# A hybrid decoder layer: the gate matrix of the expert stage built eight tokens at a time, with its products on GpSimd and ScalarE

## The chip, the cores and the metric

The kernel runs on one core of one Trainium2 chip. Its time is the device time of one execution in microseconds (us). The kernel before took 3386.84 us (median of three runs, 3384.8 to 3387.58). The five engines of the core are TensorE (PE in the profile, with PEld for its weight loads), VectorE (DVE), ScalarE (ACT), GpSimd (POOL) and SyncE (SP), which here issues nearly all DMAs.

## What is computed

The reference is one decoder layer on 512 tokens of width 2048: modulation, a short convolution beside differential attention, an output projection, and then a product-key expert layer (PEER), which is where the change lies. For every token it picks 8 x 16 of 16384 one-neuron experts:

```
idx = jnp.take_along_axis(cand_idx, top_p, axis=-1)      # 128 experts of a token
g   = jax.nn.softmax(top_s.astype(jnp.float32), axis=-1)
a   = jnp.einsum('thkd,td->thk', jnp.take(expert_u, ib, axis=0), xb)
w   = gelu(a) * gb
out = jnp.einsum('thk,thkd->td', w, jnp.take(expert_v, ib, axis=0))
```

All arithmetic that the change touches is in float32.

## The kernel before, in words

The kernel treats the first 160 tokens of the expert layer (TG) by gathering their experts' rows, and the other 352 (TD) densely: it computes the activations of all 16384 experts for them, multiplies each by its gate (zero for experts not chosen) and multiplies with all rows of expert_v. An expert's number is 128 times a high part plus a low part, so the gates of one token are a 128 x 128 matrix, G = sum over its 128 picks of onehot(high) x gate x onehot(low).

**The gate-matrix stage (lines 914 to 938)** makes G for the 352 dense tokens, in 11 blocks of 32 (GB). `opT[i]` holds, with the 128 picks on the partitions, the high part, the low part and the gate of every token; `iof` is the row 0..127. Four tokens at a time: VectorE compares `iof` with both parts (line 924, 2 x 4 x 128 elements, into a `gt` tile of which there are three); two tokens' one-hots of the high part are multiplied by the gates on VectorE (line 927) and two on ScalarE (line 930), into `og` (three buffers); TensorE multiplies the two one-hot matrices of each token (line 933, one float32 product shows as two instructions in the trace); ScalarE moves the four results out of PSUM into `gtile` (line 934; two buffers), and after 32 tokens SP stores the block to `g_dram` (line 935).

**What runs beside it.** `u_block(e)` (line 790) makes the activations of 128 experts: 48 matrix products per block (line 798). Its rows come from `u_dram`, in a half-block `u_turn` (line 777): SP loads `ur` (line 783), VectorE transposes it for blocks from 12 on (line 786), and `split` makes a high and a low half, on ScalarE (line 88) and VectorE (line 89). Blocks 0 to 3 lie before the stage, 4 to 11 belong to it. `lay_out` (line 224) issues DMAs from one place in DRAM to another, `u_dram`, 256 KB each, which have been put behind a gate product in the program's order only. The blocks need no gate matrix. The first products with expert_v (line 963) do: they take W, which `w_block` (line 823) makes from a reload of `g_dram` (line 826), over all 11 stores.

**The order of the work** on each engine is fixed when the program is built: a scheduler interleaves the stage and the blocks by its own estimate of times, under the dependencies and the explicit orders. Each engine then goes through its row in that order. PSUM has eight banks: in this stage two for the blocks (psA) and six for `pv` (psV).

Of the kernel before, what the change touches and what calls it, by code (L numbers as in the profile page):

```python
# [57 lines left out]
OG_BUFS = 3  # L58
# [20 lines left out]
def hymba_peer(tc, x, c, positions, w_ada, b_ada, norm1_g, w_in, conv_w, q_norm_g, k_norm_g,  # L79
# [18 lines left out]
    with ExitStack() as ctx:  # L98
# [663 lines left out]
        psV = psV_ctx.enter_context(tc.tile_pool(name="psV", bufs=6, space=PSUM))  # L762
# [151 lines left out]
        with tc.tile_pool(name="gs", bufs=2, side="right") as gs:  # L914
            iof = gs.tile([P, P], F32, name="iof", bufs=1)
            nc.gpsimd.iota(iof, pattern=[[1, P]], base=0, channel_multiplier=0, allow_small_or_imprecise_dtypes=True)
            nb_ = TD // GB
            for b in range(nb_):
                gt_ = gs.tile([P, NK, GB], F32, name="gtile")
                for t4 in range(0, GB, 4):  # L920
                    i, tt = divmod(TG + b * GB + t4, P)
                    o = opT[i]
                    oh = gp.tile([P, D], F32, name="gt", bufs=GBUF)[:, 0:D // 2].rearrange("p (a t n) -> p a t n", a=2, n=P)
                    nc.vector.tensor_tensor(out=oh, in0=iof[:, None, None, :].to_broadcast([P, 2, 4, P]),  # L924
                                            in1=o[:, 0:2, tt:tt + 4, None].to_broadcast([P, 2, 4, P]), op=OP.is_equal)
                    og = gs.tile([P, 4, P], F32, name="og", bufs=OG_BUFS)
                    nc.vector.tensor_tensor(out=og[:, 0:2], in0=oh[:, 0, 0:2],
                                            in1=o[:, 2, tt:tt + 2, None].to_broadcast([P, 2, P]), op=OP.mult)
                    for j in (2, 3):
                        nc.scalar.activation(og[:, j], oh[:, 0, j], AF.Copy, scale=o[:, 2, tt + j:tt + j + 1])  # L930
                    pg = psV.tile([P, 4, P], F32, name="pv")
                    for j in range(4):
                        gm = nc.tensor.matmul(pg[:, j], oh[:, 1, j], og[:, j], start=True, stop=True)  # L933
                    nc.scalar.activation(gt_[:, :, t4:t4 + 4], pg.rearrange("p t n -> p n t"), AF.Copy)
                nc.sync.dma_start(g_dram[b], gt_)
                lay_out(min(2 if b % 2 else 1, len(lay)), gm)
                if b >= nb_ - (RUN - NT):
                    u_block(RUN - nb_ + b, behind=gm if b == nb_ - 1 else None)
# [134 lines left out]
```

## Time and profile before

| | us |
|---|---|
| three runs, median | 3386.84 |
| the profiled execution, its own time | 3396.71 |
| span of its instructions | 3394.6 |
| TensorE / VectorE / ScalarE / GpSimd busy | 3183.8 / 2815.8 / 1218.1 / 1002.0 |
| one gate comparison, line 924 (88 of them) | 1.218 |
| one product on VectorE, line 927 (88) | 0.416 |

The profile is that of one execution. Busy time counts an instruction from its start to its end; two neighbours on an engine overlap a little, so busy sums run above the time that the engine needs. The granted clock of TensorE over the span is 0.976 of full speed. The gate-matrix stage lies between 1281 and 1454 us. Before it, up to 1281 us, comes the choice of the experts; behind it the long loop over all experts, to the end.

### The profile page before, as it was taken

What the parts mean: (1) busy time and instruction counts of PE and PEld (TensorE: products, weight loads), DVE (VectorE), ACT (ScalarE), POOL (GpSimd) and SP (SyncE); (2) the same over time, 40 slices, a digit from 0 to 9 for tenths busy, and PEclk for the clock granted to TensorE, in tenths of its full rate; (3) what the DMA queues carried; (4) which work ended last, traced back from release to release, by engine and by line L of the source; (5) the groups of instructions that cost most, each with busy time, mean ns of one, the idle gap of its engine ahead of it and who ended that gap; (6) DMA issues with size and microseconds to landing.
All of it is one profiled execution on the core that took longest, in us unless ns stands there. A gap on an engine that the chain in (4) does not pass through costs nothing.

```text
span 3394.6 us, 47070 instructions
## 1 busy us (share of the span) xinstructions
PE 3183.8 (94%) x18006; PEld 2947.5 (87%) x18006; DVE 2815.8 (83%) x3779; ACT 1218.1 (36%) x1826; POOL 1002.0 (30%) x665
## 2 busy tenths in 40 slices
PE   4888999999999859799999999999999999999998
PEld 3766867777878649799999999999999999999997
DVE  5879767853337998978999899999999999999975
ACT  5232333343245426643233333333333333333322
POOL 2446423344445640002223222222222222222210
PEclk9999999999999979999999999999999999999999
DMA  8875978876979868888998899998988988998964
GB/s 287 277 257 174 310 247 284 271 251 203 330 248 305 281 227 305 288 314 323 350 343 336 318 339 345 349 332 330 339 323 320 345 340 325 360 331 335 347 237 168
DMA packets 388895, 1017.80 MB, mean 300 GB/s; under 512 B 29713, under 2 KB 108478, under 8 KB 328126
## 3 DMA queue, kind: packets, MB, share of 16 engines
q1 hardware_dynamic: 342590, 679.23, 59.1%
q0 software_dynamic: 46080, 335.56, 25.3%
q8 instruction: 141, 2.31, 0.3%
q14 instruction: 84, 0.69, 0.1%
HBM read 965.11 MB, written 171.18 MB: 335 GB/s over the span
## 4 chain that ended last, share of the span: by engine, by line
PE 68%; DVE 17%; DMA 9%; issue 2%; ACT 1%; SPq 1%; POOL 1%; DVEq 0%; ACTq 0%; POOLq 0%
PE pv L963 27%; PE pa L798 27%; DMA ada_w<-in_w_ada_dram 5%; PE pm L471 5%; DVE ada_acc L196 2%; PE pm L557 2%; DVE run L196 2%; DVE gt L924 2%; PE pm L257 2%; PE pm L712 1%; DMA wraw<-in_w_out_dram 1%; PE pv L933 1%; DVE tkj L687 1%; PE sp L425 1%; DVE cv L674 1%
## 5 line engine op out<-in xcount | busy, mean ns | idle before, releaser
L798 PE MATMUL pa<-hd,ut 128*128 128x352 f32 x6144 | 1066.7, 326 | 28.7 <-DVE ut L89 21.7
L963 PE MATMUL pv<-W,vs 128*128 128x352 f32 x6144 | 1049.0, 324 | 5.8 <-ACT W L88 2.6
L798 PEld LDWEIGHTS pa<-hd,ut 128*128 128x128 f32 x6144 | 1007.3, 190 | 33.6 <-DVE ut L89 24.3
L963 PEld LDWEIGHTS pv<-W,vs 128*128 128x128 f32 x6144 | 997.9, 188 | 9.3 <-ACT W L88 3.5
L89 POOL TENSOR_TENSOR wsp<-wraw,wsp 128x1024 fp32r<-128x1024 f32 x160 | 393.6, 2464 | 559.3 <-ACT wsp L88 524.5
L88 ACT ACTIVATE vs<-vr 128x1024 fp32r<-128x1024 f32 x256 | 271.6, 1061 | 741.8 <-PE pv L963 694.8
L852 POOL DMA_INDIRECT gt<-in_expert_u_dram,idxu x128 | 181.7, 1419 | 724.4 <-DVE gt L860 318.8
L860 DVE SCALAR_TENSOR_TENSOR gt<-gt,h2n 128x2048 f32<-128x2048 f32 x160 | 364.3, 2281 | 14.9 <-DMA gt<-in_expert_u_dram,idxu 14.9
L88 ACT ACTIVATE ut<-ur 128x1024 fp32r<-128x1024 f32 x256 | 269.5, 1055 | 296.6 <-PE pa L798 229.5
L873 DVE SCALAR_TENSOR_TENSOR gacc<-gt,ga_a,gacc 128x2048 f32<-128x2048 f32 x158 | 369.5, 2339 | 3.0 <-DMA gt<-in_expert_v_dram,idxu 2.2
L89 DVE TENSOR_TENSOR vs<-vr,vs 128x1024 fp32r<-128x1024 f32 x256 | 310.7, 1214 | 53.4 <-ACT vs L88 53.0
L89 DVE TENSOR_TENSOR ut<-ur,ut 128x1024 fp32r<-128x1024 f32 x256 | 310.4, 1216 | 46.8 <-ACT ut L88 45.9
L852 POOL DMA_INDIRECT gt<-in_expert_v_dram,idxu x128 | 175.2, 1369 | 551.1 <-DVE gacc L873 382.1
L88 ACT ACTIVATE wsp<-wraw 128x1024 fp32r<-128x1024 f32 x160 | 169.1, 1058 | 389.5 <-issue 94.7
L471 PE MATMUL pm<-big,wsp 128*128 128x512 f32 x1152 | 286.5, 401 | 0.0
L786 DVE STREAM_TRANSPOSE ur<-ur 128x1024 f32<-128x1024 f32 x232 | 274.4, 1219 | 10.6 <-DMA ur<-u_dram 10.6
L471 PEld LDWEIGHTS pm<-big,wsp 128*128 128x128 f32 x1152 | 215.3, 192 | 42.9
L196 DVE SCALAR_TENSOR_TENSOR ada_acc<-ada_w,scol,ada_acc 128x512 f32<-128x512 f32 x195 | 208.1, 1067 | 39.0 <-DMA ada_w<-in_w_ada_dram 35.0
L257 PE MATMUL pqk<-wsp,big 128*128 128x512 f32 x768 | 192.0, 409 | 22.4 <-DVE qk L303 14.5
L712 PE MATMUL pm<-big,wsp 128*128 128x512 f32 x768 | 187.3, 401 | 19.5 <-POOL wsp L89 17.9
L257 PEld LDWEIGHTS pqk<-wsp,big 128*128 128x128 f32 x768 | 149.5, 198 | 58.6 <-DVE qk L303 17.4
L712 PEld LDWEIGHTS pm<-big,wsp 128*128 128x128 f32 x768 | 146.1, 193 | 52.5 <-POOL wsp L89 20.9
(271 smaller groups left out, 3045.1 us busy)
## 6 DMA issues: line engine op xcount, KB each, us to landing
ur<-u_dram SPq DMA_DIRECT2D x128, 1024.0 KB
vr<-in_expert_v_dram SPq DMA_DIRECT2D x256, 512.0 KB
u_dram<-in_expert_u_dram SPq DMA_DIRECT2D x464, 256.0 KB
ada_w<-in_w_ada_dram SPq DMA_DIRECT2D x192, 512.0 KB
wraw<-in_w_in_dram SPq DMA_DIRECT2D x96, 512.0 KB
g_dram<-gtile SPq DMA_DIRECT2D x11, 2048.0 KB
g<-g_dram SPq DMA_DIRECT2D x32, 704.0 KB
wraw<-in_w_out_dram SPq DMA_DIRECT2D x32, 512.0 KB
```

The source lines that it names most:

```text
L88: hi = nc.scalar.activation(dst[:, 0], src, AF.Copy)
L89: (eng or nc.vector).tensor_tensor(out=dst[:, 1], in0=src, in1=dst[:, 0].bitcast(F32), op=OP.subtract)
L196: nc.vector.scalar_tensor_tensor(new, wt[:, k], s, old, op0=OP.mult, op1=OP.add)
L257: nc.tensor.matmul(banks[i], hT[kk][:, a, i * P:(i + 1) * P], ws[:, b, k], start=(kk == last[0] and n == 0), stop=(kk == last[1] and n == 2))
L471: nc.tensor.matmul(banks[n2], ws[:, a, k, n2 * P:(n2 + 1) * P], hT[kk][:, b], start=(kk == 0 and n == 0), stop=(kk == KC - 1 and n == 2))
L712: nc.tensor.matmul(banks[j], ws[:, a, k, j * P:(j + 1) * P], h2T[kk][:, b], start=(kk == 0 and n == 0), stop=(kk == KC - 1 and n == 2))
L786: nc.vector.transpose(t, t)
L798: mm = nc.tensor.matmul(pa[:, :TD], ut[:, a, j].rearrange("p b r -> p (b r)"), hd[k][:, b], start=(k == 0 and n == 0), stop=(k == KC - 1 a ...
L852: d = nc.gpsimd.indirect_dma_start(out=t, out_offset=None, in_=src, in_offset=bass.IndirectOffsetOnAxis(ap=gidx[g][:, j:j + 1], axis=0))
L860: return lambda: nc.vector.scalar_tensor_tensor(t, t, 1.0, h2n, op0=OP.mult, op1=OP.mult, accum_out=ga_a[:, j:j + 1])
L873: return lambda: nc.vector.scalar_tensor_tensor(gacc, t, a, gacc, op0=OP.mult, op1=OP.add)
L963: mm = nc.tensor.matmul(pv[j // 2][:, j % 2, :TD], vs[:, a, bb, j * P:(j + 1) * P], W[e0 // 2][:, m, bb], start=(b == 0 and n == 0), stop= ...
```

## The change

The comparison takes eight tokens at once (2 x 8 x 128 elements, the whole `gt` tile). The row `iof` is still made by GpSimd in SBUF (now `ios`), and ScalarE copies it once to a PSUM bank of its own (psI); psV goes from six banks to five. The product with the gates leaves VectorE: GpSimd does six of the eight tokens in one instruction, ScalarE two (OG_ACT), one at a time as before. `og` holds eight tokens and has two buffers instead of three. The matrix products and the way out of PSUM are the same instructions, in two groups of four per comparison, the group that holds ScalarE's tokens first.

```diff
-OG_BUFS = 3
+OG_BUFS = 2
+OG_ACT = 2
...
-        psV = psV_ctx.enter_context(tc.tile_pool(name="psV", bufs=6, space=PSUM))
+        psI = psV_ctx.enter_context(tc.tile_pool(name="psI", bufs=1, space=PSUM))
+        psV = psV_ctx.enter_context(tc.tile_pool(name="psV", bufs=5, space=PSUM))
...
-            iof = gs.tile([P, P], F32, name="iof", bufs=1)
-            nc.gpsimd.iota(iof, pattern=[[1, P]], base=0, channel_multiplier=0, allow_small_or_imprecise_dtypes=True)
+            ios = gs.tile([P, P], F32, name="ios", bufs=1)
+            nc.gpsimd.iota(ios, pattern=[[1, P]], base=0, channel_multiplier=0, allow_small_or_imprecise_dtypes=True)
+            iof = psI.tile([P, P], F32, name="iof")
+            nc.scalar.activation(iof, ios, AF.Copy)
...
-                for t4 in range(0, GB, 4):
...
-                    nc.vector.tensor_tensor(out=oh, in0=iof[:, None, None, :].to_broadcast([P, 2, 4, P]),
-                                            in1=o[:, 0:2, tt:tt + 4, None].to_broadcast([P, 2, 4, P]), op=OP.is_equal)
-                    og = gs.tile([P, 4, P], F32, name="og", bufs=OG_BUFS)
-                    nc.vector.tensor_tensor(out=og[:, 0:2], in0=oh[:, 0, 0:2],
-                                            in1=o[:, 2, tt:tt + 2, None].to_broadcast([P, 2, P]), op=OP.mult)
-                    for j in (2, 3):
+                for t8 in range(0, GB, 8):
...
+                    nc.vector.tensor_tensor(out=oh, in0=iof[:, None, None, :].to_broadcast([P, 2, 8, P]),
+                                            in1=o[:, 0:2, tt:tt + 8, None].to_broadcast([P, 2, 8, P]), op=OP.is_equal)
+                    og = gs.tile([P, 8, P], F32, name="og", bufs=OG_BUFS)
+                    m = 8 - OG_ACT
+                    nc.gpsimd.tensor_tensor(out=og[:, 0:m], in0=oh[:, 0, 0:m],
+                                            in1=o[:, 2, tt:tt + m, None].to_broadcast([P, m, P]), op=OP.mult)
+                    for j in range(m, 8):
                         nc.scalar.activation(og[:, j], oh[:, 0, j], AF.Copy, scale=o[:, 2, tt + j:tt + j + 1])
...
+                    for t4 in (4, 0):
+                        pg = psV.tile([P, 4, P], F32, name="pv")
+                        for j in range(4):
+                            gm = nc.tensor.matmul(pg[:, j], oh[:, 1, t4 + j], og[:, t4 + j], start=True, stop=True)
+                        nc.scalar.activation(gt_[:, :, t8 + t4:t8 + t4 + 4], pg.rearrange("p t n -> p n t"), AF.Copy)
```

Lines below the change move down by up to six: line 798 of before is line 800 of the changed kernel, 89 is 90, 924 is 928, 933 is 939, 786 is 788, 831 is 833.

The scheduler lays the stage out anew. TensorE's row of before, at the end of the stage (L933 is the gate product, one row count per token; L798 the products of an expert block):

```order
L933 MATMUL pv<-og,gt 128x128 x4
L798 MATMUL pa<-hd_7407,ut 128x352 x2
L933 MATMUL pv<-og,gt 128x128 x8
L798 MATMUL pa<-hd_7408,ut 128x352 x3
L798 MATMUL pa<-hd_7409,ut 128x352 x3
L933 MATMUL pv<-og,gt 128x128 x188
L798 MATMUL pa<-hd_7394,ut 128x352 x3
```

The same place in the changed kernel (L939 is the gate product, L800 the block's):

```order
L939 MATMUL pv<-og,gt 128x128 x4
L800 MATMUL pa<-hd_7403,ut 128x352
L800 MATMUL pa<-hd_7404,ut 128x352 x3
L800 MATMUL pa<-hd_7405,ut 128x352
L939 MATMUL pv<-og,gt 128x128 x4
L800 MATMUL pa<-hd_7405,ut 128x352 x2
L800 MATMUL pa<-hd_7406,ut 128x352 x3
L800 MATMUL pa<-hd_7407,ut 128x352 x3
L939 MATMUL pv<-og,gt 128x128 x8
L800 MATMUL pa<-hd_7408,ut 128x352 x3
L800 MATMUL pa<-hd_7409,ut 128x352 x3
L939 MATMUL pv<-og,gt 128x128 x31
```

Before, all seven blocks come early and the last 188 tokens stand alone; now the blocks' products are spread over the stage, 341 of them between the first gate product and the last, and 31 tokens stand alone at its end. Behind the last gate product follow 98 products of blocks before, 162 now, until the first product with expert_v.

VectorE's row of before in the middle of its tail (L924 the comparison, L927 the product, L89 the low half of a block's rows, L831 the product with the reloaded gates):

```order
L924 TENSOR_TENSOR gt<-iof,opT_10381 128x1024
L927 TENSOR_TENSOR og<-gt,opT_10381 128x256 x2
L924 TENSOR_TENSOR gt<-iof,opT_10381 128x1024 x2
L927 TENSOR_TENSOR og<-gt,opT_10381 128x256
L924 TENSOR_TENSOR gt<-iof,opT_10381 128x1024
L927 TENSOR_TENSOR og<-gt,opT_10381 128x256 x2
L89 TENSOR_TENSOR ut<-ur,ut 128x1024 x2
L831 TENSOR_TENSOR W<-W,g_12008 128x704 x2
```

VectorE's row at the end of the changed stage (L928 the comparison, L90 the low half, L788 the transposes):

```order
L928 TENSOR_TENSOR gt<-iof,opT_10384 128x2048 x3
L90 TENSOR_TENSOR ut<-ur,ut 128x1024
L928 TENSOR_TENSOR gt<-iof,opT_10384 128x2048 x3
L788 STREAM_TRANSPOSE ur<-ur 128x4x256 x2
L90 TENSOR_TENSOR ut<-ur,ut 128x1024
L928 TENSOR_TENSOR gt<-iof,opT_10384 128x2048
L90 TENSOR_TENSOR ut<-ur,ut 128x1024
L788 STREAM_TRANSPOSE ur<-ur 128x4x256 x2
L90 TENSOR_TENSOR ut<-ur,ut 128x1024 x3
L788 STREAM_TRANSPOSE ur<-ur 128x4x256 x2
L833 TENSOR_TENSOR W<-W,g_11750 128x704 x2
```

The products are gone from it, and the low halves stand between the comparisons to the end, 16 before the last comparison and two of the transposes.

GpSimd's row of the changed kernel from the last product of the choice of experts (L690) to the first gather (L854):

```order
L690 TENSOR_TENSOR tkj<-tkj,ci 128x864 x2
L918 IOTA ios 128x128
L932 TENSOR_TENSOR og<-gt,opT_10054 128x768 x12
L932 TENSOR_TENSOR og<-gt,opT_10219 128x768 x16
L932 TENSOR_TENSOR og<-gt,opT_10384 128x768 x16
L854 DMA gt<-in_expert_u_dram,idxu_9889 128x2048 x128
```

The 44 products of the gates stand where before there was nothing between the iota and the gathers.

## Rows read from the trace of the kernel before

**Rows 1.** Chain of waits, in the stage: start us, us, what ended last.
```profile
1285.43 3.75 PE pv L933 x16
...
1318.46 1.78 PE pv L933 x16
1320.24 2.10 PE pa L798 x13
...
1450.36 1.13 DVE gt L924
1451.98 2.02 PE pv L933 x16
1454.00 15.82 PE pa L798 x98
```
**Rows 2.** Stretches: length, then busy us (instructions) of PE, PEld, DVE, ACT, POOL.
```profile
1285.40:1382.00 96.60, 93.41 (x664) 93.15 (x664) 81.93 (x100) 65.72 (x146) 0.00 (x0) 0.97 0.84 304
1382.00:1454.00 72.00, 53.25 (x377) 48.65 (x378) 69.11 (x93) 52.16 (x136) 0.00 (x0) 0.93 0.82 288
```
**Rows 3.** Groups of instructions, 1281 to 1455 us: busy us, mean ns, idle before.
```profile
L924 DVE TENSOR_TENSOR gt<-iof,opT 128x1024 f32<-128x1024 f32 x88 | 105.2, 1218 | 12.8 <-PE pv L933 11.2 <-POOL iof L916 1.1
L933 PE MATMUL pv<-og,gt 128*128 128x128 f32 x704 | 97.6, 291 | 26.5 <-DVE og L927 21.9 <-ACT ut L88 4.6
...
L798 PE MATMUL pa<-hd,ut 128*128 128x352 f32 x344 | 64.3, 333 | 0.0
L930 ACT ACTIVATE og<-gt,opT 128x128 f32<-128x128 f32 x176 | 61.6, 393 | 21.2 <-DVE gt L924 19.7 <-DMA gb__9677<-gate 1.3
...
L934 ACT ACTIVATE gtile<-pv 128x512 f32<-128x512 f32 x88 | 51.8, 589 | 28.0 <-PE pv L933 27.8
L927 DVE TENSOR_TENSOR og<-gt,opT 128x256 f32<-128x256 f32 x88 | 34.4, 416 | 0.2
L89 DVE TENSOR_TENSOR ut<-ur,ut 128x1024 fp32r<-128x1024 f32 x16 | 19.5, 1217 | 2.0 <-ACT ut L88 1.9
L88 ACT ACTIVATE ut<-ur 128x1024 fp32r<-128x1024 f32 x16 | 16.7, 1050 | 1.7 <-PE pa L798 1.7
L786 DVE STREAM_TRANSPOSE ur<-ur 128x1024 f32<-128x1024 f32 x4 | 4.7, 1222 | 1.8 <-DMA ur<-u_dram 1.8
```
**Rows 4.** Groups of GpSimd over the whole span: busy us, mean ns, idle before.
```profile
L89 POOL TENSOR_TENSOR wsp<-wraw,wsp 128x1024 fp32r<-128x1024 f32 x160 | 393.6, 2464 | 559.3 <-ACT wsp L88 524.5 <-DMA u_dram<-in_expert_u_dram 15.2 <-issue 13.1
...
L689 POOL TENSOR_TENSOR tkj<-tkj,ci 128x864 f32<-128x864 f32 x32 | 70.8, 2228 | 71.0 <-DVE tkj L687 66.9 <-DVE tkf L666 4.1
...
L89 POOL TENSOR_TENSOR big<-h,big 128x512 fp32r<-128x512 f32 x16 | 20.4, 1288 | 20.9 <-ACT big L88 20.9
```
**Rows 5.** One line of VectorE: duration ns min/median/max, first and last start us.
```profile
L860 DVE SCALAR_TENSOR_TENSOR gt<-gt,h2n x160: 2243/2282/2330, 1490.7 to 3101.6; 128x2048 f32<-128x2048 f32 x160
```
**Rows 6.** The same view of a line of VectorE's and its product on GpSimd.
```profile
L687 DVE TENSOR_TENSOR tkj<-iot,tkpf x32: 1040/1050/2611, 1051.8 to 1270.9; 128x864 f32<-128x864 f32 x32
L689 POOL TENSOR_TENSOR tkj<-tkj,ci x32: 1857/1902/3727, 1053.0 to 1274.8; 128x864 f32<-128x864 f32 x32
```
**Rows 7.** Order of time from 150 us, VectorE, then GpSimd: start us, us.
```profile
149.74 0.68 DVE L303 TENSOR_TENSOR qk<-qk,pqk 128x512 f32<-128x512 f32 x1
...
151.00 1.28 DVE L303 TENSOR_TENSOR qk<-qk,pqk 128x512 f32<-128x512 f32 x2
...
149.74 2.52 POOL L89 TENSOR_TENSOR big<-h,big 128x512 fp32r<-128x512 f32 x2
```
**Rows 8.** Stretch from the first transfers of the stage; behind POOL: clock, DMA share, GB/s.
```profile
1279.40:1462.30 182.90, 156.36 (x1103) 151.09 (x1102) 157.04 (x201) 124.37 (x293) 0.24 (x1) 0.95 0.83 297
```
**Rows 9.** SP's queue in order of time: the last store of gates, their first reload.
```profile
1454.66 0.33 SPq L935 DMA_DIRECT2D g_dram<-gtile  x1
...
1462.27 0.38 SPq L826 DMA_DIRECT2D g<-g_dram  x1
```
**Rows 10.** Stretches of 100 us from 1500 us on, their sum: PE, PEld, DVE, ACT, POOL.
```profile
sum 1900.00, PE 1871.53 PEld 1862.32 DVE 1734.17 ACT 591.86 POOL 440.07; mean PE 98.50 PEld 98.02 DVE 91.27 ACT 31.15 POOL 23.16
```

More of the change, by code (lines that the diff above doesn't have):

```diff
@@ L919, in hymba_peer @@
                 gt_ = gs.tile([P, NK, GB], F32, name="gtile")
-                for t4 in range(0, GB, 4):
-                    i, tt = divmod(TG + b * GB + t4, P)
+                for t8 in range(0, GB, 8):
+                    i, tt = divmod(TG + b * GB + t8, P)
                     o = opT[i]
-                    oh = gp.tile([P, D], F32, name="gt", bufs=GBUF)[:, 0:D // 2].rearrange("p (a t n) -> p a t n", a=2, n=P)
-                    nc.vector.tensor_tensor(out=oh, in0=iof[:, None, None, :].to_broadcast([P, 2, 4, P]),
-                                            in1=o[:, 0:2, tt:tt + 4, None].to_broadcast([P, 2, 4, P]), op=OP.is_equal)
-                    og = gs.tile([P, 4, P], F32, name="og", bufs=OG_BUFS)
-                    nc.vector.tensor_tensor(out=og[:, 0:2], in0=oh[:, 0, 0:2],
-                                            in1=o[:, 2, tt:tt + 2, None].to_broadcast([P, 2, P]), op=OP.mult)
-                    for j in (2, 3):
-                        nc.scalar.activation(og[:, j], oh[:, 0, j], AF.Copy, scale=o[:, 2, tt + j:tt + j + 1])
[L931 to L934, printed above, removed]
@@ new lines, in hymba_peer @@
+                    oh = gp.tile([P, D], F32, name="gt", bufs=GBUF).rearrange("p (a t n) -> p a t n", a=2, n=P)
+                    nc.vector.tensor_tensor(out=oh, in0=iof[:, None, None, :].to_broadcast([P, 2, 8, P]),
[4 more added lines that the diff above has]
+                                            in1=o[:, 2, tt:tt + m, None].to_broadcast([P, m, P]), op=OP.mult)
```

## The prediction, made before the changed kernel ran

> **What bounds the kernel now.** I read the chain of waits first, then the gate-matrix stage by stretches and by groups, and last what stands beside it on GpSimd and in the transfers. The stage has two halves. In the chain, the first is TensorE alone: gate products and block products follow each other without a gap, 16 of the one in 1.78 us, 13 of the other in 2.10 us. Towards the end the chain lies on VectorE's comparison instead, and only the last products and the 98 of the block behind it are TensorE's again [rows 1]. The stretches say the same: up to 1382 us TensorE is busy 93.4 of 96.6 us; from 1382 to 1454 us VectorE is busy 69.1 of 72, TensorE shows 53.3 (by starts and ends that overlap), and GpSimd does nothing in either [rows 2]. In the groups TensorE's idle time before a gate product is 26.5 us, 21.9 of it ended by VectorE's product of line 927 [rows 3].
>
> What TensorE needs at its own pace is 1.78/16 = 0.111 us for a gate product and 2.10/13 = 0.1615 us for a block product. From 1285.43 us, the first gate product, to 1454.00 + 15.82 = 1469.82 us it does 704 of the one (78.3 us) and 344 + 98 = 442 of the other (71.4 us): 149.7 us of work in 184.4 [rows 1, 3]. The stage thus holds 34.7 us in which TensorE waits, and 30 of them lie in the tail, where the 188 tokens that stand alone in the order are 376 x 0.111 = 41.8 us of work in 72. Behind the stage there is little to be had: 28.5 us of TensorE idle in the 1900 us from 1500 us on [rows 10].
>
> **The change part by part.** *VectorE's products go.* 88 x 0.416 us [rows 3] leave the engine that sets the tail's pace. In the chain a comparison of 1.218 us costs 1.13, since neighbours overlap by 0.09 [rows 1, 3]; I take that 0.09 off every duration on VectorE.
>
> *The comparison takes eight tokens.* No row shows it. An instruction of 2048 elements on two SBUF inputs takes 2.28 us [rows 5]; the step from 864 elements (1.050 us) to 1024 (1.218 us) is 1.05 ns each, which gives 2.29 for 2048 [rows 3, 6]. A PSUM input costs nothing more: 512 elements with one take 0.68 us [rows 7], and 1.050 less 352 x 1.05 ns is 0.68 as well. So 2.28, or 2.19 by spacing, against 2 x 1.13; a dearer PSUM input is bounded by the fourth rival. With 16 low halves at 1.217 - 0.09 and two transposes before the last comparison, VectorE has 44 x 2.19 + 18 x 1.13 = 96.4 + 20.3 = 116.7 us of work in the stage.
>
> *GpSimd's product* of 768 elements: below, line 689's shortest in proportion, 1.857 x 768/864 = 1.65 us [rows 6]; above, the line through 512 elements (1.288) and 1024 (2.464) gives 1.88, and 3.1 if one low half of 1.22 us is waited out [rows 3, 4]. I take 1.8, near the undisturbed rows: 44 x 1.8 = 79 us on an engine that is empty.
>
> *The lock between the two engines.* When VectorE's comparison of line 687, with both inputs in SBUF, meets its product on GpSimd, it takes up to 2.611 us instead of 1.040, and the product up to 3.727 instead of 1.857 [rows 6]. When its input lies in PSUM, it doesn't: line 303 ran once at 0.68 us and twice at 0.64 beside 2.52 us of GpSimd's work [rows 7]. So the new comparison stays free and the 16 low halves, with two SBUF inputs, do not. A product fills 1.8 of some 3.03 us per eight tokens (below), so a low half waits 0.59 x 0.9 = 0.53 us on average: 8.5 us, between 0 and 16 x 1.8 = 28.8. VectorE then has 125 us.
>
> The Trainium skill, page "SBUF — State Buffer", section "Who interferes with whom", states this as a rule: an instruction of VectorE's with two SBUF inputs and one of GpSimd's that reads SBUF exclude each other for the whole instruction, one with a single SBUF input does not take part. The trace agrees on both sides (2.611 against 1.040 us; 0.68 unchanged). By that rule the PSUM row is what the change lives on: with it the sum is the forecast's, without it the fourth rival's.
>
> *ScalarE* keeps 88 moves out of PSUM (0.589) and 16 high halves (1.050), and has 88 products instead of 176 (0.393): 51.8 + 16.8 + 34.6 = 103 us [rows 3]; the one copy of the row costs one such product, 0.4 us, at the start.
>
> *TensorE* has the same work, now spread: 704 x 0.111 + 341 x 0.1615 = 78.3 + 55.1 = 133.4 us up to the last gate product, 3.03 per eight tokens, with a block's products between the groups. That is the largest of the four sums, so TensorE becomes the bound. What it still waits: at the start up to 2.8 us (copy 0.4, longer comparison 1.07, product 1.8 instead of 0.42), of which I take 1.5, since its first product waited on ScalarE's queue in any case [rows 3]; the lock, 0 to 16 us there, of which I take 7; the 31 tokens alone at the end, 3.9 comparisons at 2.19 against 1.78, 1.5. Together 10 us instead of 34.7: a gain of 24.7.
>
> *What is late next.* The reload of the gates is issued 7.6 us after the last store [rows 9], and the first product with expert_v follows 15.8 us after the last gate product, covered by 98 block products [rows 1]. Now 162 x 0.1615 = 26.2 us cover it, 10 more. One PSUM bank fewer and two `og` buffers of eight tokens instead of three of four I cost at nothing: a buffer is held for 1.8 us of product and about 3 of TensorE, 4.8 in the 6.06 that two periods give; without that 1.2 us of reserve each low half's wait would pass on to TensorE, which is the upper end above.
>
> **The sum.** Against the profiled execution, 3396.71 us (span 3394.6): 3396.7 - 24.7 = 3372. The median of the runs lies 9.9 us lower, so the prediction for it is 3386.84 - 24.7 = 3362. With TensorE's waits between 3 and 17 us the likeliest case reaches from 3355 to 3369.
>
> **The rivals.** *First: the lock makes VectorE the bound.* If every low half waits out a whole product, VectorE has 116.7 + 28.8 = 145.5 us, more than TensorE; with 2.8 at the start and 1.6 at the end the stage to the last gate product takes 150 instead of 168.6: 18.6 less, 3368. For it: line 687's mean in the choice of experts must hold such waits, as its longest shows. Against it: most of its 32 cases stand at 1.05 (the median) [rows 6].
>
> *Second: the transfers.* From 1279.4 to 1462.3 us the DMA engines are busy 0.83 of 182.9 us, 151.8 us [rows 8]. Nothing of that goes, so the forecast, with the reload 24.7 us earlier, wants 151.8 in 158.2 us, 96%. At 90% the reload comes after 168.7 us, 14 earlier: 3373. For it: stores, block rows and lay-outs share SP's one row, and a late block row stops TensorE. Against: the 10 us of cover behind the last gate product, and the 17% of the stretch that are free today.
>
> *Third: the long loop gives it back.* The order is rebuilt to the end of the program; if the loop's 28.5 us of TensorE idle [rows 10] came to 53, nothing would be left: 3387. Against it: the same work and the same engines in the same proportions.
>
> *Fourth: slower.* If the PSUM row does not free the comparison from GpSimd's product (broadcast operands, unlike line 303's), the two alternate: 2.19 + 1.8 = 3.99 us per eight tokens, 44 x 3.99 + 18 x 1.13 = 196 us against 168.6 now: 27 us slower, 3414. It decides from (168.6 - 20.3)/44 = 3.37 us per eight tokens on. Rows 7 speak against it.
>
> **How the numbers follow.** Forecast 0.54, first rival 0.17, second 0.13, third 0.09, fourth 0.07. A measurement of this kernel tells about 0.2%, 6.8 us, from no change. The first three cases are faster by more, except some 0.02 of weaker transfers, half of it no change and half slower: faster 0.82, no change 0.10, slower 0.08. The range reaches from a stage with no wait left (34.7 gained, 3352, and a microsecond for the loop) to 3384, past the transfers' case and into the third's: 3351 to 3384.
>
> **What would show it.** Right: in the changed profile 44 comparisons at 2.28 us and 44 products on GpSimd at 1.7 to 2.2 us; the last gate product 143 to 145 us after the first; TensorE's idle time before gate products near 10 us instead of 26.5; low halves with some durations near 3 us. Wrong: comparisons well above 2.3 us (fourth rival), TensorE waiting for block rows with the DMA engines above 0.95 (second), VectorE busy to the end of the stage with long low halves (first), or a stage that is shorter by 25 us in a span that isn't (third).

## The result and the profile after

The changed kernel takes 3355.02 us (median of six runs, 3354.14 to 3361.78) against 3386.59 for the kernel before on the same chip (six runs, 3382.88 to 3387.93): 0.9911 of the time, 95% interval 0.99 to 0.9922, 31.6 us less. The forecast was 3362. The profiled execution took 3355.41 us, with a span of 3353.6.

The chain of waits in the changed stage, columns as in [rows 1]:

```profile
1272.15 2.30 DVE gt L928
...
1276.05 3.78 PE pv L939 x16
...
1342.96 3.57 PE pv L939 x32
1346.53 2.90 PE pa L800 x18
1349.43 3.57 PE pv L939 x32
...
1409.61 2.21 DVE gt L928
...
1413.51 1.83 PE pv L939 x14
1416.37 26.16 PE pa L800 x162
```

The tail on VectorE is gone. Gate products (L939) and block products (L800) alternate on TensorE from the first comparison to the last; VectorE is on the chain again only before the last eight of the 31 tokens at the end. From the first gate product to the last the stage takes 1416.4 - 1276.0 = 140.4 us instead of 168.6. The same stretch as one row, columns as in [rows 8], then the groups of the stage from 1281 us on (without its first three comparisons), columns as in [rows 3]:

```profile
1276.00:1416.40 140.40, 137.20 (x1047) 136.85 (x1048) 116.00 (x61) 92.29 (x196) 67.38 (x43) 0.98 0.98 357
```

```profile
L928 DVE TENSOR_TENSOR gt<-iof,opT 128x2048 f32<-128x2048 f32 x41 | 92.9, 2287 | 14.9 <-PE pv L939 14.9
...
L939 PE MATMUL pv<-og,gt 128*128 128x128 f32 x686 | 84.1, 277 | 3.1 <-POOL og L932 3.1
...
L932 POOL TENSOR_TENSOR og<-gt,opT 128x768 f32<-128x768 f32 x42 | 65.9, 1569 | 69.4 <-PE pv L939 43.4 <-DVE gt L928 11.8 <-ACT gtile L940 11.4
```

TensorE is busy 137.2 of 140.4 us, VectorE 116, GpSimd 67. The direction of the waits has turned round: in [rows 3] TensorE stood 26.5 us before its gate products, mostly for VectorE (4.6 of it lie before the first one and are no part of the stage); now it stands 3.1, while the comparison waits 14.9 and GpSimd's product 43.4 us for TensorE to let go of a buffer. Minimum, median and maximum of the two new instructions, columns as in [rows 5]:

```profile
L928 DVE TENSOR_TENSOR gt<-iof,opT x44: 2280/2285/2293, 1272.2 to 1409.5; 128x2048 f32<-128x2048 f32 x44
L932 POOL TENSOR_TENSOR og<-gt,opT x44: 1469/1472/2369, 1274.5 to 1412.0; 128x768 f32<-128x768 f32 x44
```

**Where the time went**, counted over equal work. Before, TensorE did 704 gate and 434 block products from 1285.43 to 1469.82: the two stretches of [rows 2] hold 664 + 377 = 1041 products, 704 of gates and 337 of blocks (one of them counted at the edge, seven blocks of 48 are 336), and 98 follow. The prediction has 344 for the 336, a count from 1281 to 1455 us that takes in products outside the stage. The work is thus 78.3 + 434 x 0.1615 = 148.4 us in 184.4, and 36.0 us were waits, where the prediction has 34.7. Now it takes 1416.37 - 1276.05 = 140.3 us for 704 and 341, and 93 of the 162 block products behind, 93 x 0.1615 = 15.0: 155.3 us, 6.9 of them waiting. That is 29.1 us. What follows takes 3353.6 - 1431.4 = 1922.2 us, and took 3394.6 - 1469.8 = 1924.8: another 2.6. The sum is 31.7. The two profiled executions lie 9.4 us further apart than that, 1285.4 against 1276.1 at the start of the stage: the profiled execution of before is 9.9 us above its median.

SP's queue after the stage, columns as in [rows 9]:

```profile
1417.03 0.33 SPq L941 DMA_DIRECT2D g_dram<-gtile  x1
...
1426.47 0.39 SPq L828 DMA_DIRECT2D g<-g_dram  x1
```

The reload follows the last store by 9.4 us instead of 7.6. The first product with expert_v starts at 1442.4, 26.0 us behind the last gate product, and block products fill all of that.

### The profile page after: what moved, and what is told of

The parts are those of the page before. It is cut to its first block, busy times and chain, and to the rows that moved or that the text cites. A ratio compares the mean times of both kernels' runs of the same rounds, so it can differ in the third digit from the quotient of the medians.

```text
span 3353.6 us, 46956 instructions
## 1 busy us (share of the span) xinstructions
PE 3169.9 (95%) x18006; PEld 2940.8 (88%) x18006; DVE 2780.9 (83%) x3647; ACT 1192.6 (36%) x1739; POOL 1080.5 (32%) x709
## 4 chain that ended last, share of the span: by engine, by line
PE 72%; DVE 16%; DMA 8%; issue 2%; ACT 1%; SPq 1%; POOL 1%; DVEq 0%; ACTq 0%; POOLq 0%
PE pa L800 28%; PE pv L969 28%; PE pm L472 5%; DMA ada_w<-in_w_ada_dram 4%; PE pv L939 2%; PE pm L558 2%; DVE ada_acc L197 2%; DVE run L197 2%; PE pm L258 2%; PE pm L713 1%; DMA uar<-in_expert_u_dram 1%; DVE tkj L688 1%; PE sp L426 1%; DMA wraw<-in_w_out_dram 1%; DVE cv L675 1%
## 5 line engine op out<-in xcount | busy, mean ns | idle before, releaser
L800 PE MATMUL pa<-hd,ut 128*128 128x352 f32 x6144 | 1065.3, 325 | 25.3 <-DVE ut L90 20.7
L800 PEld LDWEIGHTS pa<-hd,ut 128*128 128x128 f32 x6144 | 1005.9, 189 | 29.0 <-DVE ut L90 22.9
L90 POOL TENSOR_TENSOR wsp<-wraw,wsp 128x1024 fp32r<-128x1024 f32 x160 | 393.8, 2465 | 547.8 <-ACT wsp L89 502.9
L89 ACT ACTIVATE vs<-vr 128x1024 fp32r<-128x1024 f32 x256 | 271.6, 1061 | 742.7 <-PE pv L969 691.6
L89 ACT ACTIVATE ut<-ur 128x1024 fp32r<-128x1024 f32 x256 | 270.0, 1056 | 315.0 <-PE pa L800 255.6
L854 POOL DMA_INDIRECT gt<-in_expert_u_dram,idxu x128 | 185.3, 1447 | 548.6 <-DVE gt L862 314.6
L90 DVE TENSOR_TENSOR ut<-ur,ut 128x1024 fp32r<-128x1024 f32 x256 | 310.5, 1217 | 60.0 <-ACT ut L89 58.9
L90 DVE TENSOR_TENSOR vs<-vr,vs 128x1024 fp32r<-128x1024 f32 x256 | 311.4, 1217 | 54.3 <-ACT vs L89 53.3
L854 POOL DMA_INDIRECT gt<-in_expert_v_dram,idxu x128 | 178.3, 1393 | 543.9 <-DVE gacc L875 364.1
L89 ACT ACTIVATE wsp<-wraw 128x1024 fp32r<-128x1024 f32 x160 | 169.1, 1058 | 388.8 <-issue 92.7
L472 PE MATMUL pm<-big,wsp 128*128 128x512 f32 x1152 | 281.4, 396 | 0.0
L788 DVE STREAM_TRANSPOSE ur<-ur 128x1024 f32<-128x1024 f32 x232 | 274.3, 1220 | 4.7 <-DMA ur<-u_dram 4.5
L472 PEld LDWEIGHTS pm<-big,wsp 128*128 128x128 f32 x1152 | 211.7, 188 | 41.6
L713 PE MATMUL pm<-big,wsp 128*128 128x512 f32 x768 | 187.1, 401 | 18.4 <-POOL wsp L90 16.8
L558 PE MATMUL pm<-big,wsp 128*128 128x512 f32 x768 | 182.3, 397 | 9.5 <-ACT wsp L89 6.0
```

Of the source, the lines that this page charges most:

```text
L89: hi = nc.scalar.activation(dst[:, 0], src, AF.Copy)
L90: (eng or nc.vector).tensor_tensor(out=dst[:, 1], in0=src, in1=dst[:, 0].bitcast(F32), op=OP.subtract)
L472: nc.tensor.matmul(banks[n2], ws[:, a, k, n2 * P:(n2 + 1) * P], hT[kk][:, b], start=(kk == 0 and n == 0), stop=(kk == KC - 1 and n == 2))
L558: nc.tensor.matmul(banks[j], ws[:, a, k, j * P:(j + 1) * P], yT[kk0 + k][:, b], start=(kq == 0 and k == 0 and n == 0), stop=(kq == 7 and k ...
L788: nc.vector.transpose(t, t)
L800: mm = nc.tensor.matmul(pa[:, :TD], ut[:, a, j].rearrange("p b r -> p (b r)"), hd[k][:, b], start=(k == 0 and n == 0), stop=(k == KC - 1 a ...
```

## The experiments

Three chips were used; the kernel before took 3385.93 us on the first (23 runs), 3386.05 on the second (17) and 3382.77 on the third (11). "Stage" is the time from the first gate product's start to the last one's end, in one profiled execution (before 168.6, the changed kernel 140.3).

| kernel | chip | median us (runs) | against before | stage us |
|---|---|---|---|---|
| row in SBUF | 1 | 3390.78 (12) | 1.0018 [1.0006, 1.0029] | 170.3 |
| batches of eight, products on VectorE | 1 | 3366.40 (5) | 0.9939 [0.9926, 0.9952] | 153.5 |
| no product on VectorE | 1 | 3363.43 (5) | 0.9933 [0.992, 0.9945] | 148.8 |
| order only | 1 | 3383.87 (11) | 0.9989 [0.998, 0.9998] | 166.8 |
| order only, rows not late | 2 | 3381.48 (11) | 0.9986 [0.9976, 0.9995] | 161.3 |
| four at a time | 2 | 3365.33 (6) | 0.9941 [0.9925, 0.9958] | 152.2 |
| three og buffers | 2 | 3354.97 (5) | 0.991 [0.9896, 0.9925] | 140.3 |
| four tokens on ScalarE | 2 | 3361.78 (6) | 0.9928 [0.9912, 0.9943] | 137.6 |
| one token on ScalarE | 3 | 3358.39 (5) | 0.9927 [0.9914, 0.994] | 141.8 |
| no token on ScalarE | 3 | 3372.01 (5) | 0.9962 [0.9949, 0.9975] | 141.8 |
| changed kernel once more | 3 | 3360.59 (6) | 0.9938 [0.9924, 0.9951] | 140.1 |

The theory: VectorE gives up its products, the PSUM row keeps its comparison out of GpSimd's way, and TensorE becomes the bound. The rivals: the PSUM row does nothing; or the new order alone, with the blocks spread over the stage, is the gain.

### The row stays in SBUF

```diff
-            iof = psI.tile([P, P], F32, name="iof")
+            iof = gs.tile([P, P], F32, name="iof", bufs=1)
```

> The changed kernel with the row 0..127 copied to an SBUF tile instead of a PSUM bank; TensorE's order is the same row by row. Lock theory: the comparison now has two SBUF inputs and excludes GpSimd's product, so the two alternate: 2.19 + 1.47 = 3.66 us per eight tokens, 44 x 3.66 + 18 x 1.13 = 181 us for the stage instead of 140, about 41 more than the changed kernel: 3396, slower than before; comparisons or products in the trace at 3.5 to 3.8 us. Rival (no lock between these two): 3355, durations unchanged at 2.28 and 1.47.

Measured: 3390.78 us, 5 us slower than before. TensorE's row is the changed kernel's, instruction for instruction. The groups of the stage:

```profile
L931 POOL TENSOR_TENSOR og<-gt,opT 128x768 f32<-128x768 f32 x43 | 128.3, 3006 | 37.6 <-DVE gt L927 29.0 <-PE pv L938 8.7
L927 DVE TENSOR_TENSOR gt<-iof,opT 128x2048 f32<-128x2048 f32 x42 | 126.4, 3052 | 0.4 <-PE pv L938 0.3
L938 PE MATMUL pv<-og,gt 128*128 128x128 f32 x702 | 91.9, 286 | 25.7 <-POOL og L931 25.3
...
L90 DVE TENSOR_TENSOR ut<-ur,ut 128x1024 fp32r<-128x1024 f32 x17 | 40.0, 2360 | 10.3 <-ACT ut L89 10.3
```

and the comparison and the product alone:

```profile
L927 DVE TENSOR_TENSOR gt<-iof,opT x44: 2277/3551/3559, 1274.3 to 1442.1; 128x2048 f32<-128x2048 f32 x44
```

```profile
L931 POOL TENSOR_TENSOR og<-gt,opT x44: 1467/3359/3515, 1276.6 to 1444.5; 128x768 f32<-128x768 f32 x44
```

The shortest cases are the changed kernel's (2.28 and 1.47); the medians are 1.27 and 1.89 us longer. Each of the two waits for the other inside its own duration, TensorE's wait moves back to 25 us, now for GpSimd, and the low halves (L90) double as well. The row's place is worth 30 us of the stage (170.3 against 140.3), and 27 to 36 us of the whole time: 4.9 us slower than before here, 22.2 and 31.6 us faster in the two measurements of the changed kernel. That is more than the whole change. The forecast's fourth rival is what happens without the PSUM row. The lock theory held, with a price too high: it asked for 181 us of stage and 3396. The rule of the Trainium skill that the prediction leaned on, page "SBUF — State Buffer", section "Who interferes with whom", says that an instruction of VectorE's with two SBUF inputs contends with one of GpSimd's that reads SBUF, and that one with a single SBUF input does not. The trace agrees on both sides (3.55 against 2.285 us).

### Batches of eight alone

The comparison takes eight tokens, but the row stays in SBUF and VectorE multiplies four of eight tokens in one instruction; GpSimd does nothing here.

```diff
+OG_ACT = 4
...
-            iof = psI.tile([P, P], F32, name="iof")
-            nc.scalar.activation(iof, ios, AF.Copy)
+            iof = ios
...
-                    nc.gpsimd.tensor_tensor(out=og[:, 0:m], in0=oh[:, 0, 0:m],
+                    nc.vector.tensor_tensor(out=og[:, 0:m], in0=oh[:, 0, 0:m],
```

> Eight tokens per comparison, but the row in SBUF and the products divided as before (four of eight on VectorE in one instruction, four on ScalarE), GpSimd idle. VectorE's sum in the stage is 44 x (2.19 + 0.59) + 20.3 = 143 us against 150 before. Relief theory (only VectorE's work counts): 7 us gained, 3379. Order theory (the blocks' products, which the scheduler spreads here too but for 82 tokens at the end, are what counts): TensorE 115 us, then 10.25 x 2.78 = 28.5 for the tail and some 3 of waits, 147 instead of 168.6: 3365. If batching does nothing: 3386.

Measured: 3366.40, 19.5 us faster than before. The comparison, the product, and the stage as one row:

```profile
L926 DVE TENSOR_TENSOR gt<-ios,opT x44: 2280/2285/2294, 1264.0 to 1413.6; 128x2048 f32<-128x2048 f32 x44
```

```profile
L930 DVE TENSOR_TENSOR og<-gt,opT x44: 649/684/694, 1270.6 to 1416.4; 128x512 f32<-128x512 f32 x44
```

```profile
1266.90:1420.60 153.70, 142.79 (x1048) 140.15 (x1049) 144.60 (x107) 116.83 (x286) 0.00 (x0) 0.96 0.90 325
```

With both inputs in SBUF and nothing on GpSimd the comparison takes the same 2.285 us, so the PSUM row is neither dearer nor cheaper by itself. VectorE's work hardly shrinks (44 x 0.684 = 30.1 us of products instead of 36.6), and it is busy 144.6 of 153.7 us, yet most of the change's gain is there: the relief theory, which had asked for 3379, was wrong on this one, and the order theory's 3365 comes near. The scheduler now leaves 82 tokens alone at the end instead of 188. Of the 15.1 us by which the stage is shorter, 6.4 are VectorE's work (151.0 us in the stage of before); the rest is idle time of VectorE's, 17.6 us before and 9.1 here.

### No product on VectorE, all else as before

This kernel leaves out VectorE's products: two of every four tokens get no gates, and their high one-hots go to TensorE as they are.

```diff
-                    nc.vector.tensor_tensor(out=og[:, 0:2], in0=oh[:, 0, 0:2],
-                                            in1=o[:, 2, tt:tt + 2, None].to_broadcast([P, 2, P]), op=OP.mult)
...
-                        gm = nc.tensor.matmul(pg[:, j], oh[:, 1, j], og[:, j], start=True, stop=True)
+                        gm = nc.tensor.matmul(pg[:, j], oh[:, 1, j], oh[:, 0, j] if j < 2 else og[:, j], start=True, stop=True)
```

> The kernel before with VectorE's products left out: two of every four tokens go into the matrix product without their gates. GpSimd stays idle, comparisons of four tokens. VectorE's sum falls to 88 x 1.13 + 20.3 = 120 us, below TensorE's 133; the order has 144 tokens alone at the end (36 groups at 1.13). Relief theory: nearly the changed kernel's gain: 100.6 + 40.7 + 2 = 143 instead of 168.6, 3361. Order theory (a long tail alone costs whatever VectorE does): under half the gain, 3372 or more.

Measured: 3363.43, 22.5 us faster. The relief of VectorE by itself, at four tokens a comparison and with the order that the scheduler then makes, is worth some two thirds of the change. 144 tokens stand alone at the end of this order.

### The order alone

The code of before, with the block products of blocks 4 to 10 held, in the program's order only, behind evenly spaced gate products:

```diff
+                        if 4 <= e <= 10 and j % 4 == 0 and n == 0 and gms:
+                            at = ((e - 4) * 4 + q * 2 + j // 4) * len(pending) // 28
+                            tc.add_manual_dep(mm.ins, gms[min(at, len(gms) - 1)].ins.name, ORDER, reason="spread")
```

> The kernel before with the same instructions, but the block products of blocks 4 to 10 tied by order alone behind gate products, so that they stand spread through the stage, 12 between every 12 tokens, with 32 tokens alone at the end. VectorE still has 150 us of work. Relief theory in its strict form: no change, 3386. Order theory in its strict form: TensorE's 133 us and the changed kernel's few us of wait, 3357. Both count: the stage can't be shorter than VectorE's 150 and some 3 us of waits, 153 instead of 168.6: 3371.

Measured: 3383.87, 2 us less than before on that chip. Its profile has a hole that the edit made, in the chain of waits:

```profile
1414.42 1.23 DVE ut L89
1415.67 9.38 DMA ur<-u_dram
1425.11 1.13 issue
1426.24 1.20 DVE ur L787
1427.44 2.31 DVE gt L928 x3
```

The rows of block 12 come late, its transpose waits for them, and comparisons stand behind that transpose in VectorE's row. A second kernel puts these transposes behind the last comparison:

```diff
+                if 24 <= n < 28:
+                    tc.add_manual_dep(tr.ins, cmps[-1].ins.name, ORDER, reason="behind the last comparison")
```

> The order-only kernel, in which VectorE stood 11 us before the transposes of block 12 (rows that landed late) with three comparisons and their products queued behind; here those transposes are also tied behind the last comparison, still nothing but order. If both order and VectorE's work count: VectorE's 150 us and some 5 of waits instead of 167, so 3384 - 12 = 3372. If order gives nothing whatever stands behind VectorE's waits: 3384 again.

Measured: 3381.48, 4.6 us less than before on its chip. Its stage:

```profile
1270.90:1432.10 161.20, 142.52 (x1041) 137.24 (x1042) 149.96 (x191) 115.89 (x281) 0.00 (x0) 0.98 0.87 314
```

The blocks are spread, the hole is gone, and VectorE is busy 150 of 161 us. The stage is 7.3 us shorter than before, though only 32 tokens stand alone; the median gains 4.6 us, 1.7 to 8.1 by its interval, and not the 12 that both causes together had been given. So spreading the blocks without taking work from VectorE gives some quarter of the gain at the most; it is not what the gain rests on.

### Four tokens at a time, with GpSimd and the PSUM row

```diff
-                for t8 in range(0, GB, 8):
+                for t8 in range(0, GB, 4):
...
-                    og = gs.tile([P, 8, P], F32, name="og", bufs=OG_BUFS)
-                    m = 8 - OG_ACT
+                    og = gs.tile([P, 4, P], F32, name="og", bufs=OG_BUFS)
+                    m = 4 - OG_ACT
```

The rest is the changed kernel's, with OG_ACT at 1 and three og buffers.

> The changed kernel with four tokens per comparison: row in PSUM, three products of four on GpSimd in one instruction, one on ScalarE, og of four tokens and three buffers. VectorE has 88 x 1.13 + 20.3 = 120 us, 3 more than with eight. The scheduler's order leaves 176 tokens alone at the end. Relief theory: 176 x 0.2225 + 54.3 = 93.5 us for the mixed part, 44 x 1.13 = 50 for the tail and 3 of waits, 146 us, so some 3361 to 3364. If the eight tokens themselves are needed (fewer waits between engines): 3375 or more.

Measured: 3365.33, 20.7 us faster than before, 10 us short of the changed kernel's 3355.02 (and of the 3354.97 with a third og buffer, below, on the same chip). GpSimd's product in this kernel:

```profile
L932 POOL TENSOR_TENSOR og<-gt,opT x88: 827/828/1857, 1273.5 to 1424.5; 128x384 f32<-128x384 f32 x88
```

It waits 76.0 us for comparisons. 176 tokens are left alone at the end here, where TensorE goes at VectorE's pace. So the batch of eight carries the last third. How, is an estimate: four tokens alone take 1.13 us of VectorE and 0.89 of TensorE, so 176 cost 44 x 0.24 = 10.6 us, against 1.6 for the 31 of the changed kernel; that is 9.0 of the 11.9 us between the two stages.

### How many tokens on ScalarE, and a third og buffer

```diff
-OG_BUFS = 2
+OG_BUFS = 3
```

> The changed kernel with three og buffers instead of two. GpSimd waited 43.4 us for matrix products in the changed kernel, most of it for a free og; but TensorE is the bound there. If that is so: no change from 3355 (3352 to 3358). If the buffers hold the stage back: up to its remaining 7 us, 3348.

Measured: 3354.97 and a stage of 140.3 us, both those of the changed kernel, in an order of TensorE's that differs in places (345 block products in the stage instead of 341). GpSimd's 43 us of waiting for a free buffer cost nothing: TensorE is the bound.

```diff
-OG_ACT = 2
+OG_ACT = 4
```

> The changed kernel with four of eight products on ScalarE and four on GpSimd. ScalarE's sum rises from 103 to 88 x 0.59 + 16 x 1.05 + 176 x 0.39 = 137 us, just above TensorE's 133; GpSimd's falls from 65 to some 45. If the largest sum sets the stage: 4 to 8 us longer, 3359 to 3363. If GpSimd's latency before a matrix product is what TensorE still waits for: 3350 to 3353.

Measured: a stage of 137.6 us, 2.7 shorter, but 3361.78 in all. That is the first theory's time, for another reason than it gave: the stage did not grow. Behind the stage the chain of waits leaves TensorE:

```profile
1439.75 1.68 DVE W L833 x2
1441.43 2.27 DVE vs L90 x2
1443.70 1.60 DVE W L90 x2
```

The first product with expert_v starts at 1445.5, 33 us behind the last gate product instead of 26. In between (1434 to 1442) TensorE is busy 6.1 of 8 us at a granted clock of 0.79; it waits 2.2 us for the halves of a block's rows, which ScalarE and VectorE had made late. Over equal work the gain of the stage is gone by then. The further 7 us that this kernel is slower lie behind that product; where they come from stays open.

```diff
-OG_ACT = 2
+OG_ACT = 1
```

> The changed kernel with seven products on GpSimd (1.7 us) and one on ScalarE; the order leaves 72 tokens alone, 9 comparisons. By the same count 3 us more than the changed kernel: 3356 to 3359. If ScalarE's shorter row lets it serve the moves out of PSUM sooner: 3350 to 3354.

Measured: 3358.39, the same as the changed kernel on that chip (3360.59, below) within the intervals; the 3 us more that the count had asked for did not come.

```diff
-OG_ACT = 2
+OG_ACT = 0
```

> The changed kernel with all eight products on GpSimd, 1.9 us by the slope between 384 (0.83) and 768 elements (1.47), none on ScalarE. The sums stay under TensorE's 133 (GpSimd 84, VectorE 117, ScalarE 69), but the order leaves 96 tokens alone at the end, 12 comparisons at 2.2 to 2.3 against TensorE's 1.78: 5 us more than the changed kernel's: 3359 to 3361. If only the sums count: 3355. If the two og buffers of eight tokens no longer cover 1.9 us of product and the matrix products: 3365 or more.

Measured: 3372.01, a miss. With GpSimd's product of all eight tokens the stage is 141.8 us, as with seven, so the loss of some 12 us lies outside it. Its profiled execution starts the stage 3.6 us later than the one with one token on ScalarE, and TensorE is busy 794 of the 800 us from 2400 on where the changed kernel's is busy 799. Why an order so like the other loses there stays open.

### The operands of GpSimd's product

The changed kernel with fifteen more products of 768 elements on GpSimd, three each of five kinds of operands; a single run, 3361.47 us, which isn't a measure of the change.

```diff
+            for out_, a_, b_ in ((sc, sa, sb), (sc, sa, per_row), (sc, sa, per_col), (sc, sc, per_col), (sc, sc, sb)):
+                for _ in range(3):
+                    nc.gpsimd.tensor_tensor(out=out_, in0=a_, in1=b_, op=OP.mult)
```

> The changed kernel with 15 further products of 768 elements on GpSimd between the first real ones, three each of: two full inputs; a full input and one value per partition and token (the shape of the changed kernel's product); a full input and one row repeated for all six tokens (the shape of line 689); the last two also written in place. The prediction took 1.8 us from products of other shapes; 1.47 came. Theory: the operand with one value for 128 elements is cheaper: 1.75 to 1.9 for two full inputs, 1.47 for the value, 1.65 for the row. Rival: the rows of before were long only for what ran beside them: all 1.47. The time says nothing (some 20 us longer).

GpSimd in order of time (start us, us), of each kind one that VectorE did not hold up: two full inputs first, then one value per partition and token (as in the kernel), then one row repeated, then in place:

```profile
1277.26 1.81 POOL L928 TENSOR_TENSOR sc<-h2n 128x768 f32<-128x768 f32 x1
...
1285.29 1.47 POOL L928 TENSOR_TENSOR sc<-h2n,opT 128x768 f32<-128x768 f32 x1
...
1293.77 1.85 POOL L928 TENSOR_TENSOR sc<-h2n,opT 128x768 f32<-128x768 f32 x1
...
1301.22 1.82 POOL L928 TENSOR_TENSOR sc<-sc,opT 128x768 f32<-128x768 f32 x1
```

An input that holds one value for 128 elements makes the product 1.47 us; two full inputs 1.81; a repeated row also 1.8. Right on the first, wrong on the repeated row, which had been expected between.

### The changed kernel once more

> The changed kernel once more, on this chip, beside the other divisions of the products: 3355 (3353 to 3362).

Measured on the third chip: 3360.59 against 3382.77, 22.2 us faster (0.9938, [0.9924, 0.9951]) instead of 31.6. The stage is the same, 140.1 us. The profiled execution is 5.4 us longer than that of the first measurement: 1.2 of it before the stage, and most of the rest at the program's end, where TensorE has gaps and its granted clock falls in places. Two of the stretches of 10 us there, the changed kernel first, then this run (PE's busy time is the second number, the granted clock the third from the end):

```profile
3293.60:3303.60 10.00, 7.75 (x38) 6.84 (x38) 5.03 (x17) 1.61 (x6) 0.00 (x0) 0.83 0.16 55
```

```profile
3299.00:3309.00 10.00, 8.12 (x34) 7.47 (x34) 4.57 (x12) 0.57 (x3) 0.00 (x0) 0.66 0.16 56
```

As a mean of 2.4 and 1.2 GHz, 0.83 is a third of the stretch at the lower one and 0.66 two thirds. Summed over the last 150 us in stretches of 10, what the clock takes from full speed is 6.6 us in the first and 10.7 in the second. That is an estimate of 4.1 us of the 5.4, and an upper one, since TensorE also stands in these stretches. So the gain is 22 to 32 us by chip and run; its part in the stage repeats.

## Why the prediction was right, and which terms were off

- **TensorE becomes the bound: right.** It is busy 137.2 of 140.4 us, a third buffer changes nothing, and the engines around it wait for it. The stage was forecast at 143 to 145 us from the first gate product to the last and took 140.3. The time, 3355.02, lies at the lower edge of the likeliest case (3355 to 3369).
- **The comparison: right.** 2.28 forecast, 2.285 measured, and the PSUM input is free (2.285 with an SBUF row too).
- **GpSimd's product: mis-sized.** 1.8 us was taken, between bounds of 1.65 and 3.1; undisturbed it is 1.47, below the lower one. The rows used were products with two inputs of full size; the operand shapes above give 1.81 for those and 1.47 for one value per 128 elements. It was off the path but for the ends of the stage, so the sum hardly felt it.
- **The lock: on the other engine, and without a price.** 8.5 us of stretched low halves on VectorE were forecast, 7 of them for TensorE. The low halves between the comparisons, columns as in [rows 5]:

```profile
L90 DVE TENSOR_TENSOR ut<-ur,ut x15: 1181/1225/1227, 1279.9 to 1408.4; 128x1024 fp32r<-128x1024 f32 x15
```

  None is stretched. It is GpSimd's product that waits, nine times, up to 2.37 us instead of 1.47 and some 4 us in all, on an engine that is idle half the time. The traces show what decides: within the stage, the one of the two that starts first takes its own time, and the other, started while it runs, waits until it ends. In the changed kernel all low halves start while GpSimd stands idle. With a third og buffer ten of them start while a product runs. One case of each, VectorE and GpSimd in order of time, the changed kernel first:

```profile
1297.34 1.23 DVE L90 TENSOR_TENSOR ut<-ur,ut 128x1024 fp32r<-128x1024 f32 x1 [1.57 <-ACT ut L89]
1297.88 2.02 POOL L932 TENSOR_TENSOR og<-gt,opT 128x768 f32<-128x768 f32 x1 [2.66 <-ACT gtile L940]
```

```profile
1297.12 1.47 POOL L932 TENSOR_TENSOR og<-gt,opT 128x768 f32<-128x768 f32 x1 [0.66 <-DVE gt L928]
1297.84 1.83 DVE L90 TENSOR_TENSOR ut<-ur,ut 128x1024 fp32r<-128x1024 f32 x1 [0.80 <-PE pv L939]
```

  In that kernel the ten low halves take 1.81 to 2.49 us, 8.2 us more than undisturbed: the 8.5 that had been forecast for VectorE. Its stage is 140.3 us all the same. So the step that failed is the one from VectorE to TensorE, the 7 us: VectorE had the room for them.
- **TensorE's waits: 10 forecast, 6.9 measured,** and made up otherwise. The start, the middle and the end of the stage as stretches:

```profile
1276.00:1283.10 7.10, 7.05 (x36) 7.05 (x37) 7.10 (x5) 4.02 (x9) 3.84 (x2) 0.57 0.89 260
...
1300.00:1400.00 100.00, 100.00 (x778) 100.00 (x777) 85.55 (x44) 67.45 (x144) 49.76 (x32) 1.00 0.99 374
...
1409.00:1416.40 7.40, 4.26 (x36) 4.07 (x35) 2.81 (x2) 2.74 (x6) 1.47 (x1) 1.00 1.01 341
```

  In the middle nothing is left to gain. At the start the granted clock is 0.57, most of it at 1.2 GHz, after 14 us in which TensorE was busy 9.1: 7.1 x 0.43 = 3.1 us that are no wait for another engine. At the end 3.1 us go by before the last tokens, whose comparison stands behind a low half. The prediction gave 3 to both ends together and 7 to the lock; the ends are dearer and the lock is free, so that 10 and 6.9 lie as near each other as they do is luck. (Before, the first 16 products took 3.75 us as well [rows 1], so the waits of before held such a stretch too.)
- **The loop behind: 0 forecast, 2.6 us gained.** No run settles where; it is less than the 4.3 us by which two executions of the changed kernel differ behind the stage. With the 3.1 us between 10 and 6.9 and the 1.3 that the count of block products had left out of the waits of before, this makes up the difference between 24.7 and 31.6.
- **The profiled execution of before was 9.9 us above its median**, and the prediction's way of subtracting the gain from the median was right: the difference of the two profiles, 41 us, would have been wrong by that.

Of the rivals, the first (VectorE as the bound) fell: it is busy 116 of 140 us. The second's condition came true and its price did not: the DMA engines are busy 0.98 of the stage, and 0.95 of the stretch up to the reload, where 96% had been worked out, and TensorE still waited for no rows, since the block products behind the stage are many and run without a gap to the first product with expert_v. The third fell. The fourth is what the kernel would do with the row in SBUF, though cheaper than priced (3391 instead of 3414, a stage of 170 us instead of 196): the product is 1.47 us and not 1.8, which is 44 x 0.33 = 14.5 us of it.

What the prediction did not take apart is how the gain comes about. VectorE's work enters twice: it sets the pace at which tokens that stand alone pass, and the stage can't be shorter than its sum (150 of 161 us with 32 tokens alone). How many stand alone is the scheduler's doing: 188 before, 176 and 144 in the four-token kernels, 82 with batches of eight on VectorE, 31 in the change. The runs don't show what it goes by; it isn't VectorE's work alone, which is the same with one and no token on ScalarE, where 72 and 96 stand alone. There eight tokens alone take 2.19 us of VectorE against TensorE's 1.78, and the stage is 1.5 us longer than the changed kernel's. Order alone gave 2 to 5 us, relief of VectorE at four tokens a comparison 21 to 23, batches of eight with VectorE's products 20, all together 32; these are medians of kernels that each have their own order, so they need not add up.

## What to carry to other kernels

When an engine's work is moved to GpSimd, ask first what the neighbour on VectorE reads: with both inputs in SBUF the same move made this kernel slower, and one row copied once to PSUM was worth 27 to 36 us. Read a stage's gain over equal work, not from the difference of two profiles, and find out from the trace which engine paces the part of the order where the other work has run out. A buffer or a split that is tuned further behind the new bound (a third og buffer, other shares for ScalarE) gives nothing, or hands back behind the stage what it gains within.

## What the hardware showed unexpectedly

- GpSimd's product depends on the operand, not only on the size: 768 float32 elements take 1.47 us when one input holds one value per 128 elements, and 1.81 us with two full inputs or with a repeated row, in place or not; 384 elements of the first kind take 0.83 us.
- GpSimd's product and a low half on VectorE (two SBUF inputs) don't share the time: in the stage the one that starts first keeps its duration (1.47 or 1.23 us), and the other waits for its end (up to 2.48 us for the product, 2.49 for the low half, both in the kernel with three og buffers).
- VectorE's comparison of 2048 elements takes 2.285 us whether its row lies in PSUM or in SBUF; only GpSimd's presence separates them, 3.55 against 2.285.
- The DMA engines were busy 0.98 of the stage, at 357 GB/s against 297 in [rows 8], and the bound engine didn't notice.
